# Hybrid decoder layer on one core: expert down products moved behind their own gate products, and the end of the last layer norm shared out anew

## Chip, cores and metric

One Trainium2 chip, of which the program uses one core. The metric is the time of one execution on the device in microseconds (us); lower is better. What a measurement of this kernel can tell from no change is given in the prediction.

## What is computed

The reference is one decoder layer over 512 tokens of width 1024, in float32. Attention and a spatial gating unit feed an output projection, then `x <- LN(alpha*x + mix)`. The part that this case is about comes after it: a mixture of 32 experts, of which each token uses two, and the second layer norm.

```python
def hierarchical_moe(h, ...):
    # top-1 of 4 groups, then top-2 of its 8 experts: gate (tokens, groups, experts), two entries a token
    y = jnp.zeros((B * S, D), jnp.float32)
    for g in range(N_GROUPS):
        gu = jnp.einsum('td,edf->tef', t, w_gate_up[g])
        a, b = gu[..., :EXPERT_FF], gu[..., EXPERT_FF:]
        act = jax.nn.silu(a) * b * gate[:, g, :, None]
        y = y + jnp.einsum('tef,efd->td', act, w_down[g])
    return y
...
h = layer_norm(DEEPNORM_ALPHA * h + moe, ln2_g, ln2_b)    # mean, variance, scale, shift over 1024
```

## The kernel before

**Expert pairs.** The 32 experts are worked off as 16 pairs. Each expert has 64 places for tokens, so a pair fills the 128 partitions. The weights of a pair are six tiles of 1 MB: four for the gate and up product (two halves of the depth for each of the two experts) and two for the down product. All 96 tiles come in this order over SP's queue into a ring of 20 slots (`wfill`, `slots`, L499 to L529). A slot is filled again as soon as its last product is through; up to eight transfers are under way, and SP issues the next when the eighth before it has landed.

**One turn of the loop over pairs** (L1136 to L1161) for pair p. `gate_up` (L894) multiplies gathered tokens by the gate and up weights in eight steps k; steps 0 to 3 need the first two tiles, 4 to 7 the other two. Between the steps stands other work: at k 1 the activation of pair p-1 is transposed (`act_transposed`, L1080), at k 3 `down(p - 1)` (L1089) multiplies it by the down weights, at k 4 and 5 the tokens of pair p+1 are transposed (L1071), at k 5 `fetch` picks and gathers the tokens of pair p+3. After the loop `gated` (L1074) makes silu(a)*b*gate on ScalarE and VectorE. So the down product of a pair runs in the middle of the next pair's gate products, from the down tiles that came before them. Only for the last pair, 15, `down(14)` is done before the gate products.

**Rows out and back.** ScalarE copies one half of a pair's down result out of PSUM and VectorE the other (L1101); GpSimd then writes the rows to a DRAM scratch `y_dram` by an indirect transfer (L1107): plane 0 for a token's first expert, plane 1 for its second. After the loop both planes are read back, four blocks of 128 tokens, eight transfers of 512 KB on SP (L1168); they wait for the rows of pair 14.

**The end.** Pair 15 does not go through DRAM. Its result is kept as a rounded part and a rest, `y`, and a one-hot matrix `G` spreads it over the tokens. Per block of 128 tokens and half of the width TensorE adds up in one PSUM bank: x (`fin_x`, L1197), pair 15 (`fin_y`, L1201) and the sum of the two planes (`fin_rows`, L1209). VectorE adds the planes (L1206) and takes their row sum with it. The mean of a row is put together from three sums: that of x (L1155, one block in each of pairs 11 to 14), that of pair 15 (L1238) and that of the planes (L1206, L1207). Then `ln2_scale`: ScalarE squares both halves with the mean as bias (L1214) and takes the root of the variance (L1215, L1216), VectorE subtracts the mean and multiplies by the gain (L1218). `ln2_out`: VectorE takes the reciprocal (L1222), multiplies and adds the shift (L1225), SP writes the result. Gain and shift are spread over 128 partitions by four products with 4 rows (L1175), loaded as a small tile `lnr` (L1142).

TensorE's order is written out by hand, as are those of VectorE, ScalarE, GpSimd and SP from the output projection on; waits follow from the tiles.

Of the kernel before, what the change touches and what calls it, by code (L numbers as in the profile page):

```python
# [21 lines left out]
S = 512  # L22
# [9 lines left out]
SUMMED = (NPAIR - 1,)  # L32
# [24 lines left out]
def layer(tc, I, out):  # L57
# [1031 lines left out]
    def down(p, aT, dp=None):  # L1089

        dp = dp or [ps_acc() for _ in range(2)]
        y = [wk.tile([128, D], F32R, name="y", bufs=2) for _ in range(2 if p in SUMMED else 1)]
        for n in range(2):
# [6 lines left out]
            if p not in SUMMED:  # L1100
                (dve.tensor_copy if n else act.copy)(y[0][:, ns].bitcast(F32), dp[n])  # L1101
            else:
                act.activation(y[0][:, ns], dp[n], AF.Copy, accum_out=rs[:, 2 * n:2 * n + 1])
                dve.scalar_tensor_tensor(y[1][:, ns], dp[n], 1.0, y[0][:, ns].bitcast(F32), op0=ALU.mult, op1=ALU.subtract,
                                         accum_out=rs[:, 2 * n + 1:2 * n + 2])
        if p not in SUMMED:
            pool_e.indirect_dma_start(out=y_dram[:, :], out_offset=bass.IndirectOffsetOnAxis(ap=tos[p][:, 0:1], axis=0),  # L1107
                                      in_=y[0].bitcast(F32), in_offset=None, bounds_check=2 * S - 1, oob_is_err=False)
        wfill(6 * p + 6 + NSLOT)
        return y  # L1110
# [60 lines left out]
    ln2 = slots[0]().rearrange("p (a d) -> p a d", a=2)  # L1171
    ln2_g, ln2_b = ln2[:, 0], ln2[:, 1]
    for j in range(4):
        b = ps_t().rearrange("p a b -> p (a b)")
        pe.matmul(b, ident[0:4, j:j + 1].to_broadcast([4, 128]), lnr[0:4], start=True, stop=True)  # L1175
        act.copy(ln2[:, j // 2, j % 2 * 512:j % 2 * 512 + 512], b)
    aT = act_transposed(sa)

# [7 lines left out]
    rs = mo.tile([128, 4], F32, name="rs")  # L1186
# [149 lines left out]
```

## Time and profile before

| | |
|---|---|
| three timed runs | 516.08, 517.49, 517.2 us, median 517.2 us |
| profiled execution | 520.19 us, of which 518.5 us from the first to the last instruction (the span) |
| busy share of the span | TensorE 92%, VectorE 44%, ScalarE 29%, GpSimd 23% |
| chain that ended last | TensorE 57%, transfers 31% (gate and up weights alone 20%), VectorE 7% |
| transfers | 141.18 MB, 272 GB/s over the span, 411 to 425 GB/s in slices 22 to 35 of the 40 (272 to 454 us) |

The times of the rows count from the first instruction of the profiled execution. Such an execution is longer than a timed run, so differences are worked out within it and then set against the median. PE is TensorE, PEld its weight load, DVE VectorE, ACT ScalarE, POOL GpSimd, SPq the queue of the sync engine. The granted clock is TensorE's: 1.00 is 2.4 GHz, 0.50 is 1.2 GHz. A float32 product of 128x512 shows as two records.

### The profile page before, as it was taken

What the parts mean: (1) busy time and instruction counts of PE and PEld (TensorE: products, weight loads), DVE (VectorE), ACT (ScalarE), POOL (GpSimd) and SP (SyncE); (2) the same over time, 40 slices, a digit from 0 to 9 for tenths busy, and PEclk for the clock granted to TensorE, in tenths of its full rate; (3) what the DMA queues carried; (4) which work ended last, traced back from release to release, by engine and by line L of the source; (5) the groups of instructions that cost most, each with busy time, mean ns of one, the idle gap of its engine ahead of it and who ended that gap; (6) DMA issues with size and microseconds to landing.
All of it is one profiled execution on the core that took longest, in us unless ns stands there. A gap on an engine that the chain in (4) does not pass through costs nothing.

```text
span 518.5 us, 6540 instructions
## 1 busy us (share of the span) xinstructions
PE 476.4 (92%) x2314; PEld 280.3 (54%) x2314; DVE 229.1 (44%) x588; ACT 150.4 (29%) x321; POOL 117.5 (23%) x186
## 2 busy tenths in 40 slices
PE   6999999999799999979999999999979799689971
PEld 4788887888677678769443333333313233133440
DVE  2586648624667457995532222222212322020166
ACT  4543446241668423123111111111101110012241
POOL 4024443000478511243111111111101110002000
PEclk9999999999989999998899999999979999799897
DMA  8734221930595478594589999999999999984513
GB/s 266 265 119 123 82 82 40 300 106 0 187 417 139 165 234 334 203 361 166 178 328 411 424 417 417 420 422 420 418 423 425 419 421 421 425 371 149 227 40 126
DMA packets 40748, 141.18 MB, mean 272 GB/s; under 512 B 10455, under 2 KB 14595, under 8 KB 28936
## 3 DMA queue, kind: packets, MB, share of 16 engines
q1 hardware_dynamic: 35816, 130.72, 65.8%
q0 software_dynamic: 4896, 10.00, 5.4%
q8 instruction: 20, 0.33, 0.2%
q14 instruction: 16, 0.13, 0.1%
HBM read 131.78 MB, written 16.25 MB: 286 GB/s over the span
## 4 chain that ended last, share of the span: by engine, by line
PE 57%; DMA 31%; DVE 7%; SPq 1%; issue 1%; ACT 1%; DVEq 0%; ACTq 0%
DMA wc<-in_w_gate_up 20%; PE acc L898 9%; PE acc L318 7%; PE acc L320 7%; PE acc L319 7%; PE acc L1099 5%; DMA wc<-in_w_down 4%; DMA wc19b<-in_w_down 4%; PE acc L913 3%; DMA x_sb<-in_x 2%; PE tp L613 2%; PE acc L598 1%; PE acc L573 1%; PE acc L575 1%; PE acc L574 1%
## 5 line engine op out<-in xcount | busy, mean ns | idle before, releaser
L898 PE MATMUL acc<-wc,xTm 128*64 128x512 f32 x456 | 126.6, 618 | 12.7 <-DMA wc<-in_w_gate_up 12.5
L898 PEld LDWEIGHTS acc<-wc,xTm 128*64 128x64 f32 x456 | 31.9, 139 | 68.8 <-issue 49.8
L318 PE MATMUL acc<-w_hi,xTh 128*128 128x512 f32 x160 | 64.9, 406 | 2.0 <-ACT w_hi L309 1.1
L319 PE MATMUL acc<-w_lo,xTh 128*128 128x512 f32 x160 | 62.8, 393 | 0.5 <-DVE w_lo L310 0.5
L320 PE MATMUL acc<-w_hi,xTl 128*128 128x512 f32 x160 | 62.8, 392 | 0.0
L1099 PE MATMUL acc<-wc,aT 128*64 128x512 f32 x248 | 57.7, 593 | 0.5 <-ACT aT L1086 0.5
L1101 DVE COPY y<-acc 128x512 f32<-128x512 f32 x15 | 10.4, 692 | 107.8 <-PE acc L1099 107.8
L1107 POOL DMA_INDIRECT y_dram<-y,to x15 | 15.1, 1009 | 157.3 <-DVE y L1101 157.3
L310 DVE TENSOR_TENSOR w_lo<-w_raw,w_hi 128x512 fp32r<-128x512 f32 x40 | 28.2, 706 | 35.8 <-ACT w_hi L309 35.6
L309 ACT ACTIVATE w_hi<-w_raw 128x512 fp32r<-128x512 f32 x40 | 25.3, 632 | 54.6 <-PE acc L320 47.9
L1099 PEld LDWEIGHTS acc<-wc,aT 128*64 128x64 f32 x248 | 18.1, 137 | 36.9 <-issue 36.2
L420 POOL TENSOR_TENSOR P<-P,st 128x128 f32<-128x128 f32 (+3 forms) x32 | 23.3, 748 | 52.3 <-DVE st L419 50.7
L318 PEld LDWEIGHTS acc<-w_hi,xTh 128*128 128x128 f32 x160 | 30.2, 189 | 9.1 <-ACT w_hi L309 1.8
L319 PEld LDWEIGHTS acc<-w_lo,xTh 128*128 128x128 f32 x160 | 30.1, 188 | 6.9 <-DVE w_lo L310 1.4
L320 PEld LDWEIGHTS acc<-w_hi,xTl 128*128 128x128 f32 x160 | 30.0, 188 | 6.8 <-DVE xTl L161 0.4
L1072 ACT COPY xTm<-tp 128x512 f32<-128x512 f32 x15 | 8.8, 587 | 68.1 <-PE tp L1071 68.1
L1071 PEld LDWEIGHTS tp<-ident,xg 128*128 128x128 f32 x120 | 15.5, 193 | 23.5 <-issue 13.0
L890 POOL DMA_INDIRECT xg<-h_dram,ti x15 | 15.7, 1049 | 44.7 <-issue 22.9
L866 DVE TENSOR_TENSOR sel<-iota_v,slotp 128x1024 bf16<-128x1024 f32 (+2 forms) x23 | 22.5, 990 | 0.1
L1101 ACT COPY y<-acc 128x512 f32<-128x512 f32 x15 | 8.8, 586 | 46.9 <-PE acc L1099 46.9
L1077 DVE SCALAR_TENSOR_TENSOR sa<-sa,tg,acc 128x256 f32<-128x256 f32 x16 | 7.7, 480 | 32.3 <-ACT sa L1076 28.5
L1071 PE MATMUL tp<-ident,xg 128*128 128x128 f32 x120 | 21.0, 299 | 0.0
(327 smaller groups left out, 751.5 us busy)
## 6 DMA issues: line engine op xcount, KB each, us to landing
wc<-in_w_gate_up SPq DMA_DIRECT2D x61, 1024.0 KB, 20.9
wc<-in_w_down SPq DMA_DIRECT2D x31, 1024.0 KB, 19.2
w_raw<-in_w_in SPq DMA_DIRECT2D x18, 512.0 KB, 3.9
y_dram<-zeros SPq DMA_DIRECT2D x8, 512.0 KB, 8.2
wo_raw<-in_w_out SPq DMA_DIRECT2D x16, 256.0 KB, 4.3
wc<-y_dram SPq DMA_DIRECT2D x6, 512.0 KB, 5.8
x_sb<-in_x SPq DMA_DIRECT2D x8, 256.0 KB, 5.9
h_dram<-x_sb SPq DMA_DIRECT2D x4, 512.0 KB
```

Of the source, the lines that this page charges most:

```text
L309: act.activation(wh, raw, AF.Copy)
L310: dve.tensor_tensor(wl, raw, wh.bitcast(F32), op=ALU.subtract)
L318: pe.matmul(acc[i], xh, wh, start=(k == 0), stop=False)
L319: pe.matmul(acc[i], xh, wl, start=False, stop=False)
L320: pe.matmul(acc[i], xl, wh, start=False, stop=(k == KD - 1))
L420: pool_e.tensor_tensor(P[:, 0:n], P[:, 0:n], bc(st4[:, 2:3], [128, n]), op=ALU.mult)
L866: dve.tensor_tensor(sels[p][:, 2 * a:2 * b], bc(iota_v.rearrange("p a b -> p (a b)")[:, None, :], [128, n, 128]), bc(slotp[:, p, a:b].rear ...
L890: pool_e.indirect_dma_start(out=xgs[p % 2], out_offset=None, in_=h_dram[:, :], in_offset=bass.IndirectOffsetOnAxis(ap=tis[p][:, 0:1], axis=0),
L898: pe.matmul(gp[zs], xT[k // 4][:, k % 4, zs], w[k % 4 // 2][:, k % 2 * 512:k % 2 * 512 + 512], start=(k == 0), stop=(k == KD - 1))
L1071: pe.transpose(out=tp[:, j], in_=xv[:, kk * 4 + j], identity=ident)
L1099: pe.matmul(dp[n][zs], aT[:, c, zs], w[c][:, ns], start=(c == 0), stop=(c == 1))
L1101: (dve.tensor_copy if n else act.copy)(y[0][:, ns].bitcast(F32), dp[n])
```

## The change

1. From pair 9 on (`ATONCE`) `down(p)` stands right behind `gated` of the same pair p, ahead of the gate products of pair p+1. In pair 9's turn both `down(8)`, at k 3, and `down(9)`, after the loop, are done. For pairs 1 to 8 nothing moves.
2. Rows go out without their mean: for pairs 0 to 14 ScalarE copies both halves of the down result and sums them as it goes, VectorE forms minus the mean and adds it to the 1024 columns in place, then GpSimd writes the rows. x loses its mean in the same way, one block in each of pairs 9 to 12 (three VectorE instructions in place of one). So the row mean at the end is that of pair 15 alone.
3. The planes are added by GpSimd for blocks 0 to 2 (1024 columns, no sum) and by VectorE for block 3.
4. x goes into PSUM early: `fin_x(2, ...)` ahead of pair 15's gate products, `fin_x(0, 0)` and `fin_x(1, 0)` around the transposition of pair 15's activation, `fin_x(0, 1)` and `fin_x(1, 1)` behind the first `fin_y`.
5. The small tile with gain and shift is loaded by GpSimd's queue at the start of pair 14's turn, and its four products stand in pair 14's gate products, after k 6.
6. The last layer norm is reshared: for blocks 0 and 1 ScalarE multiplies by the reciprocal and GpSimd adds the shift; for blocks 2 and 3 VectorE does both, with the value in between kept in PSUM. Block 1 is scaled before VectorE adds the planes of block 3.
7. `wfill(2 + NSLOT)` is called four gate steps earlier in pair 0. SP's own list of instructions is the same at that place.

```diff
@@ pair_out, gate_up of pair 0 @@
-        if p not in SUMMED:
+        if p < LAST:
...
         gate_up(0, xT0, k, gp)
+        if k == 3:
+            wfill(2 + NSLOT)
@@ def down(p, aT, dp=None) @@
-        y = [wk.tile([128, D], F32R, name="y", bufs=2) for _ in range(2 if p in SUMMED else 1)]
+        y = [wk.tile([128, D], F32R, name="y", bufs=2) for _ in range(2 if p == LAST else 1)]
+        y0 = y[0].bitcast(F32)
+        rs = mo.tile([128, 4], F32, name="rs", bufs=2)
...
-            if p not in SUMMED:
-                (dve.tensor_copy if n else act.copy)(y[0][:, ns].bitcast(F32), dp[n])
+            if p < LAST:
+                act.activation(y0[:, ns], dp[n], AF.Copy, accum_out=rs[:, n:n + 1])
...
-        if p not in SUMMED:
+        if p < LAST:
+            dve.tensor_scalar(rs[:, 2:3], rs[:, 0:1], rs[:, 1:2], -1.0 / D, op0=ALU.add, op1=ALU.mult)
+            dve.tensor_scalar(y0, y0, rs[:, 2:3], None, op0=ALU.add)
             pool_e.indirect_dma_start(out=y_dram[:, :], ...
@@ loop over pairs @@
-        if p == LAST:
-            down(p - 1, act_transposed(sa))
+        if p == LAST - 1:
             lnr = slots[3]().rearrange("p (a d) -> p a d", a=4)[:, 0]
             for z, n in enumerate(("ln2_g", "ln2_b")):
-                sp.dma_start(out=lnr[2 * z:2 * z + 2], in_=I[n].rearrange("o (a d) -> (o a) d", a=2))
+                pool_e.dma_start(out=lnr[2 * z:2 * z + 2], in_=I[n].rearrange("o (a d) -> (o a) d", a=2))
+        if p == LAST:
+            for n in range(2):
+                fin_x(2, n)
...
-            if k == 1 and p < LAST:
+            if k == 1 and p <= ATONCE:
                 aT = act_transposed(sa)
             if k == 3:
-                if p < LAST:
+                if p <= ATONCE:
                     down(p - 1, aT)
...
-            if k == 6 and LAST - NT <= p < LAST:
-                i = p - LAST + NT
-                dve.tensor_reduce(st2[:, i, 7:8], x_sb[:, i], axis=AX.X, op=ALU.add)
+            if k == 6 and LAST - 2 - NT <= p < LAST - 2:
+                i = p - LAST + 2 + NT
+                t = st2[:, i]
+                dve.tensor_reduce(t[:, 5:6], x_sb[:, i], axis=AX.X, op=ALU.add)
+                dve.tensor_scalar(t[:, 5:6], t[:, 5:6], -1.0 / D, None, op0=ALU.mult)
+                dve.tensor_scalar(x_sb[:, i], x_sb[:, i], t[:, 5:6], None, op0=ALU.add)
...
+            if k == 6 and p == LAST - 1:
+                for j in range(4):
+                    b = ps_s()
+                    pe.matmul(b, ident[0:4, j:j + 1].to_broadcast([4, 128]), lnr[0:4], start=True, stop=True)
+                    act.copy(ln2[:, j // 2, hs[j % 2]], b)
         wfill(6 * p + 4 + NSLOT)
         sa = gated(gp, tgs[p][:, 1:2])
+        if ATONCE <= p < LAST:
+            down(p, act_transposed(sa))
@@ the end @@
+    fin_x(0, 0)
     aT = act_transposed(sa)
+    fin_x(1, 0)
...
-        dve.scalar_tensor_tensor(rb[i][0], rb[i][0], 1.0, rb[i][1], op0=ALU.mult, op1=ALU.add, accum_out=t[:, 5:6])
-        dve.scalar_tensor_tensor(t[:, 6:7], t[:, 5:6], -1.0 / D, nx[:, i:i + 1], op0=ALU.mult, op1=ALU.add)
+        if i < NT - 1:
+            pool_e.tensor_tensor(rb[i][0], rb[i][0], rb[i][1], op=ALU.add)
         for n in range(2):
-            pe.matmul(fin[i, n], ident, rb[i][0][:, hs[n]], start=False, stop=True)
+            r = rb[i][0][:, hs[n]]
+            if i == NT - 1:
+                dve.tensor_tensor(r, r, rb[i][1][:, hs[n]], op=ALU.add)
+            pe.matmul(fin[i, n], ident, r, start=False, stop=True)
...
             o = o_sb[i][:, hs[n]]
-            dve.scalar_tensor_tensor(o, o, t[:, 4:5], ln2_b[:, hs[n]], op0=ALU.mult, op1=ALU.add)
+            if i < 2:
+                act.activation(o, o, AF.Copy, scale=t[:, 4:5])
+                pool_e.tensor_tensor(o, o, ln2_b[:, hs[n]], op=ALU.add)
+            else:
+                dve.scalar_tensor_tensor(o, fin[i, n], t[:, 4:5], ln2_b[:, hs[n]], op0=ALU.mult, op1=ALU.add)
...
     ln2_out(0)
+    ln2_scale(1)
     fin_rows(3)
-    for i in range(1, NT):
+    ln2_out(1)
+    for i in (2, 3):
```

How the instructions stand on the engines that matter, at three places. TensorE from the last gate steps of pair 15 to its first down product, before (L898 gate product, L1175 gain and shift, L1084 transposition of the activation, L1197 `fin_x`, L1099 down product):

```order
L898 MATMUL acc<-wc_3609,xTm 64x512
L1175 MATMUL tp<-wc_3785,ident 128x512 x4
L1084 MATMUL sc<-ident,sa 128x128 x2
L1197 MATMUL acc<-x_sb,ident 128x512 x2
L1197 MATMUL sc<-x_sb,ident 128x512 x2
L1197 MATMUL tp<-x_sb,ident 128x512 x2
L1099 MATMUL acc<-wc_3648,aT 64x512
```

The same place now (L900, L1088, L1151 and L1105 are the lines of the gate product, the transposition, `fin_x` and the down product):

```order
L900 MATMUL acc<-wc_3653,xTm 64x512
L1151 MATMUL acc<-x_sb,ident 128x512
L1088 MATMUL sc<-ident,sa 128x128 x2
L1151 MATMUL sc<-x_sb,ident 128x512
L1105 MATMUL acc<-wc_3694,aT 64x512
```

Ten products of 512 columns stood there beside the transposition; two are left. The others stand now further ahead or behind the down product. TensorE from pair 14's last gate steps to pair 15's first, now (L1075 transposition of pair 15's tokens, L1189 the products with gain and shift):

```order
L1075 MATMUL tp<-ident,xg_2354 128x128 x4
L900 MATMUL acc<-wc_3560,xTm 64x512
L900 MATMUL acc<-wc_3562,xTm 64x512
L1189 MATMUL sc<-wc_3782,ident 128x512 x4
L1088 MATMUL sc<-ident,sa 128x128 x2
L1105 MATMUL acc<-wc_3605,aT 64x512
L1151 MATMUL tp<-x_sb,ident 128x512 x2
L900 MATMUL acc<-wc_3636,xTm 64x512
```

Before, pair 14's gate products were followed by the transposition, `down(14)` and pair 15's gate products, and held `down(13)` in their middle. Now `down(13)` stands ahead of them, and the four products and two `fin_x` lie on the way from pair 14 to pair 15. ScalarE in the last layer norm, blocks 0 and 1, before (L1214 squares, L1215 and L1216 root of the variance):

```order
L1214 ACTIVATE wc_3845,st_2628<-acc,st_2628 128x512 x2
L1215 ACTIVATE st_2628<-st_2628,eps_3846 128x1
L1216 ACTIVATE st_2628<-st_2628 128x1
L1214 ACTIVATE wc_3845,st_2628<-sc,st_2628 128x512 x2
L1214 ACTIVATE wc_3845,st_2628<-tp,st_2628 128x512 x2
```

The same now (L1235 squares, L1236 and L1237 root, L1249 multiplication by the reciprocal):

```order
L1235 ACTIVATE wc_3908,st_2628<-acc,nx 128x512 x2
L1236 ACTIVATE st_2628<-st_2628,eps_3909 128x1
L1237 ACTIVATE st_2628<-st_2628 128x1
L1249 ACTIVATE wc_3906<-wc_3906,st_2628 128x512 x2
L1235 ACTIVATE wc_3908,st_2628<-sc,nx 128x512 x2
L1235 ACTIVATE wc_3908,st_2628<-tp,nx 128x512 x2
```

Two multiplications that wait for VectorE's reciprocal now stand between the squares of one block and those of the next, for blocks 0 and 1.

## Rows read from the trace of the kernel before

**Rows 1.** Busy time by stage: stretch, length, then PE, PEld, DVE, ACT, POOL, PEclk, DMA share, GB/s.

```profile
430.00:450.00 20.00, 15.13 (x60) 4.96 (x58) 2.99 (x4) 1.93 (x4) 1.01 (x1) 0.92 1.02 422
```

**Rows 2.** Timeline of SP's queue, weight transfers: start, length, instruction.

```profile
437.29 0.33 SPq L527 DMA_DIRECT2D wc<-in_w_down  x1
448.41 0.33 SPq L527 DMA_DIRECT2D wc<-in_w_gate_up  x1
453.32 0.33 SPq L527 DMA_DIRECT2D wc<-in_w_down  x1
```

**Rows 3.** Timeline of PE, pairs 14 and 15: start, length, instruction, records, idle time before.

```profile
448.44 3.68 PE L898 MATMUL acc<-wc,xTm 128*64 128x512 f32 x6 [1.58 <-DMA wc<-in_w_gate_up]
...
458.27 1.02 PE L898 MATMUL acc<-wc,xTm 128*64 128x512 f32 x4
...
461.51 1.94 PE L898 MATMUL acc<-wc,xTm 128*64 128x512 f32 x8
...
465.50 3.65 PE L1099 MATMUL acc<-wc,aT 128*64 128x512 f32 x16 [0.52 <-ACT aT L1086]
468.98 1.46 PE L898 MATMUL acc<-wc,xTm 128*64 128x512 f32 x6
```

**Rows 4.** Timeline of PE from pair 15's last gate product to the end.

```profile
475.95 3.77 PE L1175 MATMUL tp<-wc,ident 4*128 4x512 f32 x8
...
486.93 3.65 PE L1099 MATMUL acc<-wc,aT 128*64 128x512 f32 x16
...
496.93 1.88 PE L1209 MATMUL acc<-wc,ident 128*128 128x512 f32 x4
...
498.65 1.88 PE L1209 MATMUL sc<-wc,ident 128*128 128x512 f32 x4
```

**Rows 5.** Timeline of ACT and DVE in the last layer norm.

```profile
498.00 0.69 ACT L1214 ACTIVATE wc<-acc,st 128x512 f32<-128x512 f32 x1 [6.67 <-PE acc L1209]
...
499.44 0.19 ACT L1214 ACTIVATION_READ_ACCUMULATOR wc<-acc,st 128x1 f32 x1
...
499.67 1.41 DVE L1218 SCALAR_TENSOR_TENSOR wc<-acc,st,wc 128x512 f32<-128x512 f32 x2 [2.42 <-ACT wc L1214]
...
512.18 0.15 DVE L1222 RECIPROCAL st<-st 128x1 f32<-128x1 f32 x1
512.37 1.42 DVE L1225 SCALAR_TENSOR_TENSOR wc<-wc,st,wc 128x512 f32<-128x512 f32 x2
```

**Rows 6.** Groups by shape: busy, mean ns of one, idle before.

```profile
L309 ACT ACTIVATE w_hi<-w_raw 128x512 fp32r<-128x512 f32 x40 | 25.3, 632 | 54.6 <-PE acc L320 47.9 <-DMA w_raw<-in_w_in 4.9 <-issue 1.7
L727 ACT ACTIVATE x_sb<-x_sb,mv 128x512 f32<-128x512 f32 x5 | 3.9, 808 | 0.0
L310 DVE TENSOR_TENSOR w_lo<-w_raw,w_hi 128x512 fp32r<-128x512 f32 x40 | 28.2, 706 | 35.8 <-ACT w_hi L309 35.6
L731 POOL TENSOR_TENSOR x_sb<-x_sb,ln_b 128x512 f32<-128x512 f32 x5 | 7.0, 1400 | 0.4
```

**Rows 7.** Busy time and granted clock, columns as in rows 1.

```profile
453.00:454.00 1.00, 1.00 (x6) 0.16 (x4) 0.00 (x0) 0.21 (x1) 0.00 (x0) 0.75 0.99 418
480.00:481.00 1.00, 1.00 (x5) 0.49 (x4) 0.00 (x0) 0.98 (x3) 0.00 (x0) 0.90 0.99 389
481.00:482.00 1.00, 1.00 (x3) 0.48 (x2) 0.00 (x0) 0.92 (x1) 0.00 (x0) 0.50 1.04 373
484.00:485.00 1.00, 1.00 (x3) 0.38 (x2) 0.00 (x0) 0.00 (x0) 0.00 (x0) 0.89 1.05 430
```

**Rows 8.** Transfers issued by POOL: line, count, size, median us to landing.

```profile
lb<-in_b_expert POOLq DMA_DIRECT2D x1, 16.0 KB, 6.4
y_dram<-y,to POOLq DMA_INDIRECT x15, 8.3
```

**Rows 9.** Timeline: rows of pair 14 out, and back from DRAM.

```profile
470.64 0.98 POOL L1107 DMA_INDIRECT y_dram<-y,to  x1 [9.69 <-DVE y L1101]
474.83 3.12 SPq L1168 DMA_DIRECT2D wc<-y_dram  x6
```

More of the change, by code (lines that the diff above doesn't have):

```diff
@@ L30 @@
 NPAIR = NE // 2
-SUMMED = (NPAIR - 1,)
+LAST = NPAIR - 1
+ATONCE = 9
 FF = 256
@@ L1132, in layer, with fin_x @@
     fetch(3)
-    LAST = NPAIR - 1
     st2 = mo.tile([128, NT, 8], F32, name="st2")
+    fin = {}
+    hs = [slice(0, 512), slice(512, D)]
+    def fin_x(i, n):
+        if (i, n) not in fin:
+            fin[i, n] = (ps_acc, ps_s, ps_t, ps_acc)[i]()
+            if i == 2:
+                fin[i, n] = fin[i, n].rearrange("p a b -> p (a b)")
+        pe.matmul(fin[i, n], ident, x_sb[:, i, hs[n]], start=True, stop=False)
     for p in range(1, NPAIR):
         gp = ps_acc()
-        if p == LAST:
-            down(p - 1, act_transposed(sa))
+        if p == LAST - 1:
             lnr = slots[3]().rearrange("p (a d) -> p a d", a=4)[:, 0]
             for z, n in enumerate(("ln2_g", "ln2_b")):
-                sp.dma_start(out=lnr[2 * z:2 * z + 2], in_=I[n].rearrange("o (a d) -> (o a) d", a=2))
+                pool_e.dma_start(out=lnr[2 * z:2 * z + 2], in_=I[n].rearrange("o (a d) -> (o a) d", a=2))
+            ln2 = slots[0]().rearrange("p (a d) -> p a d", a=2)
+            ln2_g, ln2_b = ln2[:, 0], ln2[:, 1]
+        if p == LAST:
+            for n in range(2):
+                fin_x(2, n)
         for k in range(KD):
@@ L1170, in layer @@
     G = one_hot(LAST)
[L1171 to L1176, printed above, removed]
+    dp = [ps_acc() for _ in range(2)]
+    fin_x(0, 0)
     aT = act_transposed(sa)
+    fin_x(1, 0)
     o2 = [slots[z]().rearrange("p (a d) -> p a d", a=2) for z in (1, 2)]
@@ L1185, in layer @@
     act.preload_act_table(AF.Sqrt)
-    rs = mo.tile([128, 4], F32, name="rs")
     nx = mo.tile([128, NT], F32, name="nx")
-    dp = [ps_acc() for _ in range(2)]
-    fin = {}
-    hs = [slice(0, 512), slice(512, D)]
-    def fin_x(i, n):
-        if (i, n) not in fin:
-            fin[i, n] = (ps_acc, ps_s, ps_t, ps_acc)[i]()
-            if i == 2:
-                fin[i, n] = fin[i, n].rearrange("p a b -> p (a b)")
-        pe.matmul(fin[i, n], ident, x_sb[:, i, hs[n]], start=True, stop=False)
     def fin_y(i, n):
@@ L1203, in fin_rows @@
     def fin_rows(i):
[L1205 to L1207 removed]
+        if i < NT - 1:
+            pool_e.tensor_tensor(rb[i][0], rb[i][0], rb[i][1], op=ALU.add)
         for n in range(2):
[L1209 removed]
+            r = rb[i][0][:, hs[n]]
+            if i == NT - 1:
+                dve.tensor_tensor(r, r, rb[i][1][:, hs[n]], op=ALU.add)
+            pe.matmul(fin[i, n], ident, r, start=False, stop=True)
     def ln2_scale(i):
         t = st2[:, i]
+        m = nx[:, i:i + 1]
         for n in range(2):
[L1214 removed]
+            act.activation(sq[:, 2 * (i % 2) + n], fin[i, n], AF.Square, bias=m, accum_out=t[:, n:n + 1])
         act.activation(t[:, 2:3], t[:, 0:1], AF.Identity, bias=eps2, scale=1.0 / D)
@@ L1224, in ln2_out @@
             o = o_sb[i][:, hs[n]]
-            dve.scalar_tensor_tensor(o, o, t[:, 4:5], ln2_b[:, hs[n]], op0=ALU.mult, op1=ALU.add)
+            if i < 2:
[3 more added lines that the diff above has]
+                dve.scalar_tensor_tensor(o, fin[i, n], t[:, 4:5], ln2_b[:, hs[n]], op0=ALU.mult, op1=ALU.add)
             sp.dma_start(out=out_d[:, i, hs[n]], in_=o)
-    for i in range(NT - 1):
-        for n in range(2):
-            fin_x(i, n)
-    y = down(LAST, aT, dp)
+    y, rs = down(LAST, aT, dp)
     for i in range(NT - 1):
         fin_y(i, 0)
+    fin_x(0, 1)
+    fin_x(1, 1)
     fin_x(NT - 1, 0)
```

12 lines of the change are left out of this document (5 added, 7 removed).

## The prediction

> **What bounds the kernel now.** I read the page first (engine shares and the 40 slices), then the busy times by stage, the chain of waits, the timelines of TensorE and of SP's queue from 430 us on, and last the timelines of ScalarE and VectorE in the final layer norm.
>
> The stages differ. From about 360 us to pair 14 the weights decide: in 20 us there TensorE is busy for 15.1, while the transfers are busy throughout [rows 1]. SP issues a weight transfer when the eighth before it has landed, so the issues date the landings: 437.3 is the landing of pair 13's last gate tile, 448.4 of pair 14's second, 453.3 of its last [rows 2]. TensorE's gate products start at 448.44, with the second tile there [rows 3]. Behind pair 14 TensorE decides: gate products of pair 15 until 475.95, 11.0 us until its down product, 10.0 us from there to the first sum with the planes [rows 4]. Then ScalarE and VectorE decide: squares from 498.00, results until 513.79 [rows 5], and 4.7 us for the last transfer and the closing.
>
> So an edit in pairs 9 to 13 is worth little by itself. What is moved on the path from the landing at 453.3 to the end is worth its full length.
>
> **Step 1, pair 14 to the end of pair 15's gate products.** Down(13) now stands ahead of pair 14's gate products. Pair 13's gate products can end 5.2 us after 437.3 (the second half of a pair's gate products takes 5.2 us with the transpositions in it, from 458.27 to 463.45). With 2.05 us from the last gate product to the down product (463.45 to 465.50) and 3.5 for it (465.50 to 468.98) [rows 3] down(13) ends at 448.0, ahead of the landing at 448.4: it costs nothing. From 453.3 the path is 5.2 (second half) + 3.7 (four products with gain and shift, from 3.77 us for eight records [rows 4]) + 2.05 + 3.5 (down(14)) + 1.7 (two `fin_x`, as long as the pair at 496.93, which is followed at 498.65 [rows 4]) + 7.0 (pair 15's gate products, 468.98 to 475.95 [rows 3, 4]). That is 23.1 us, so 476.4 against 475.95: **+0.45**. What is late next if the weights come later is the same landing.
>
> **Step 2, to the down product of pair 15.** 11.0 us before. Now 2.4: the wait of 2.05, with one `fin_x` under it, and what the second one, behind the transposition, sticks out (0.35). **−8.6**.
>
> **Step 3, to the first sum with the planes.** 10.0 us before; two `fin_x` are moved behind the first `fin_y`: **+1.7**. GpSimd's additions are taken at nothing: two times 1.40 us for 1024 columns [rows 6], 2.8 a block. Pair 14's rows leave when they did (470.6), the reads back begin at 474.8 and issue in 3.1 us [rows 9]; blocks then land about every 2.4 us (1 MB at 422 GB/s, rows 1), the first at about 482, and GpSimd ends block 0 near 485 and block 2 near 490.4, while the first sum, which needs block 0 alone, is due at 476.4 + 2.4 + 11.7 = 490.5. If that cover goes, the rows from DRAM are late next, and each us is a us.
>
> **Step 4, the last layer norm.** From the first sum to VectorE's last result 16.9 us before (496.93 to 513.79, rows 4 and 5). Now ScalarE has more to do. I count from the first sum's start: squares and sums of block 0 end at 2.7 (499.44 + 0.19 less 496.93), scaled by 4.15 (1.41 for two), reciprocal 4.3 (0.15); two multiplications on ScalarE at 0.63 each [rows 6], the nearest shape of 512 columns without a per-column operand, to 5.6; squares of block 1 to 7.25, scaled by 8.7; VectorE's two additions for block 3 at 0.71 [rows 6] to 10.1; reciprocal and two multiplications to 11.55; squares of block 2 to 13.2; then VectorE alone, two blocks of 1.41 + 0.15 + 1.42 [rows 5], to 19.2. **+2.3**. By 0.81 us for each multiplication (L727's form, rows 6) it would be 0.7 more, and with slower additions 3.3 in all; with values read from PSUM as quickly as now not under 2.2.
>
> **Step 5, the clock.** TensorE's granted clock fell to 0.50 behind the four 4-row products: 0.90 in the microsecond from 480, 0.50 in the next, and it was back in that from 484, with the engine listed as busy throughout [rows 7]. It had also been low at 453 (0.75 there), after the stall ahead of 448.44. These products now stand on the path, ahead of down(14). Some 3.4 us at half clock cost 1.7 of work; in the kernel before they fell on `fin_x`, which was on the path too, inside the 11.0 us that step 2 takes as removed. So they come back in another place: **+1.7**, between 0 (no fall) and 3.4 (a spell of twice the length, as the one that ended at 453).
>
> The Trainium skill ("TensorE: Matmul & The Clock Gate", Part 1) ties the clock to how busy the engine has been. By it, products that run without a gap would cost nothing and the sum would be 1.7 us lower; the fall at 481 behind gapless products is against that reading here.
>
> **Step 6, gain and shift.** Their two small loads stand on GpSimd's queue behind pair 13's rows, which now leave after down(13): 448.0, + 0.8 and about 1.6 (ScalarE's last copy with its sum, and VectorE's addition in place; from the 512-column forms of rows 6), and about 1 for the issue [rows 9], so 451.5. A small load of GpSimd's took 6.4 us to land, rows 8.3 [rows 8]: there at 458 to 460. TensorE wants them behind step 6 of pair 14, at 457.7 or a little later. I take **+0.5**, nearest to the 6.4 us row, which is of the same kind; bounds 0 and 3.
>
> **At nothing.** The mean of pairs 0 to 14 (VectorE twice 512 columns in place, ScalarE the second copy too): VectorE is busy 3.0 and ScalarE 1.9 of 20 us [rows 1], and nobody on the path waits for these rows but those of 13 and 14, counted above. If cover went, it would be 0.7 to 1.4 us a pair. x without its mean: three instructions on the same idle VectorE. The 2-us wait ahead of each down product of pairs 9 to 13 lies in TensorE's 4.9 us idle out of 20. The rows of pair 13 leave earlier, half a megabyte, 1.2 us of transfers at most, in the range. `wfill` moved: SP's list is the same.
>
> **Sum.** 0.45 − 8.6 + 1.7 + 2.3 + 1.7 + 0.5 = −1.95, so −2.0 us within the profiled execution (520.19 us, span 518.5), which is 3.0 us longer than the median of the three runs, 517.2. Set against the median: **515.2 us**.
>
> **The rivals.**
>
> - *The clock holds and the loads are in time.* Steps 5 and 6 fall away: −4.15, 513.0 us. For it: TensorE has fewer gaps behind 453.3 than it had. Against it: the fall at 481 [rows 7]. 0.15.
> - *The small loads arrive late, and the clock falls for long.* One mechanism at one place, in front of the four products: TensorE stands still there for up to 3 us, ahead of products that already cost it the clock, and pair 14's activation and down product and all of pair 15 wait behind it in order. Price: 2.5 more than step 6 and 1.7 more than step 5, so +2.2: 519.4 us. It decides from a landing later than about 459.5, which is 8 us after issue, less than the 8.3 us of the rows ahead in that queue [rows 8]. For it: that order of the queue. Against: 16 KB landed in 6.4. 0.22.
> - *The path is shortened but given back.* TensorE's 8.6 us return elsewhere: the rows of the planes, or the ScalarE turns in the layer norm at their upper price (+1.0), and the small loads 1 us later than step 6 has them: −2.0 + 1.0 + 1.0 = 0, 517.2 us. For it: no row shows ScalarE's multiplication by a per-row operand in this place, and GpSimd's 2.8 us a block are longer than the 2.4 between blocks. Against: the rows nearest to both are the ones that the sum uses. 0.23.
>
> A rule that speaks against the moved sums is in the Trainium skill ("SBUF — State Buffer", the "DVE blocks DMA" trap): while VectorE uses the port it shares with GpSimd, GpSimd cannot write its transfers' descriptors. By it the additions in place would delay the gathers of the next pairs by their own 0.7 to 1.4 us; no row of this case shows such a delay.
>
> **How the numbers follow.** The forecast has 0.40: between 1 and 3 us less. A measurement of this kernel can tell about 0.3%, 1.55 us, from no change. Of the forecast about 0.27 lies beyond that and 0.13 within; the first rival is faster by more (0.15); the second is slower (0.20 of 0.22 beyond the bound); the third is within, with 0.03 on the faster and 0.02 on the slower side. That gives 0.45 faster, 0.33 the same, 0.22 slower. The range of 8 in 10 goes from 512.6, the first rival with its lower bounds, to 519.0, just short of the second's centre. The likeliest case's own range is 514.2 to 516.2.
>
> **What would show it.** Step 1: the last gate product of pair 15 ends near 476.4 plus what steps 5 and 6 cost, up to 479. Step 2: its down product begins 2.4 us later. Step 3: the first sum with the planes starts 11.7 us after that, and no wait for GpSimd stands before it. Step 4: VectorE's last result 19 us after the first sum. Step 5: a granted clock of 0.50 soon after the 4-row products. Step 6: the wait ahead of these products, 0 to 3 us, put down to the two small loads. Pairs 10 to 13: waits of the gate products for transfers, as before. I would be wrong if the weights themselves came later (another rate, or SP held up), if the clock fell over a longer stretch in pairs 9 to 13, where the waits now fall between gate and down products, or if rows of pair 14 came back so late that the first sum waits.

## The result, and the profile after

| | before | changed |
|---|---|---|
| median of the timed runs | 517.2 us (515.47 to 517.49, five runs) | 522.02 us (520.48 to 522.69, five runs) |
| ratio | | 1.010, 95% interval 1.0074 to 1.0125: slower by 1% |
| profiled execution | 520.19 us, span 518.5 | 522.02 us, span 520.2 |
| busy: TensorE, VectorE, ScalarE, GpSimd | 92, 44, 29, 23% | 92, 44, 32, 25% |
| pair 15's last gate product ends | 475.95 [rows 4] | 483.96 |
| its down product begins | 486.93 [rows 4] | 486.32 |
| first sum with the planes | 496.93 [rows 4] | 498.05 |
| VectorE's last result | 513.79 [rows 5] | 516.16 |

The time was lost ahead of pair 15's last gate product. Timeline of TensorE in the changed kernel (start, length, instruction, records, idle time before), to be held against [rows 3, 4]:

```profile
452.20 1.07 PE L900 MATMUL acc<-wc,xTm 128*64 128x512 f32 x2 [0.83 <-DMA wc<-in_w_gate_up]
...
455.49 1.08 PE L900 MATMUL acc<-wc,xTm 128*64 128x512 f32 x4
458.99 6.69 PE L1189 MATMUL sc<-wc,ident 4*128 4x512 f32 x8 [2.42 <-DMA wc<-in_ln_b]
465.61 1.98 PE L900 MATMUL acc<-wc,xTm 128*64 128x512 f32 x4
...
469.83 5.27 PE L1105 MATMUL acc<-wc,aT 128*64 128x512 f32 x16 [0.52 <-ACT aT L1090]
...
476.94 7.09 PE L900 MATMUL acc<-wc,xTm 128*64 128x512 f32 x32
483.96 1.12 PE L1151 MATMUL acc<-x_sb,ident 128*128 128x512 f32 x2
...
486.32 3.65 PE L1105 MATMUL acc<-wc,aT 128*64 128x512 f32 x16
...
498.05 1.88 PE L1229 MATMUL acc<-wc,ident 128*128 128x512 f32 x4
```

TensorE stands still for 2.42 us behind the gate product of 455.49, for the shift. The four products then take 6.69 us, where the same eight records took 3.77 before [rows 4]; the last gate step takes 1.98 in place of 1.08, and down(14) 5.27 in place of 3.65. Busy time by stage of the same kernel (columns as in rows 1) shows the clock:

```profile
452.00:456.50 4.50, 4.30 (x18) 1.62 (x18) 0.69 (x1) 0.59 (x1) 0.00 (x0) 1.00 1.02 428
456.50:459.00 2.50, 0.08 (x3) 0.05 (x1) 0.00 (x0) 0.00 (x0) 0.00 (x0) 1.00 1.02 421
459.00:465.60 6.60, 6.60 (x8) 2.20 (x8) 0.00 (x0) 1.76 (x3) 0.00 (x0) 0.54 0.76 321
465.60:469.70 4.10, 2.68 (x7) 0.61 (x6) 0.48 (x1) 1.27 (x3) 0.00 (x0) 0.50 0.20 84
469.70:473.00 3.30, 3.17 (x8) 1.01 (x10) 0.00 (x0) 0.07 (x1) 0.00 (x0) 0.50 0.07 27
473.00:475.00 2.00, 2.00 (x10) 0.42 (x6) 0.00 (x0) 0.69 (x2) 0.00 (x0) 0.97 0.00 0
```

The granted clock is 1.00 up to the products, 0.50 from within them until about 473, some 13.6 us. GpSimd's timeline shows when the loads were issued:

```profile
449.63 0.99 POOL L1115 DMA_INDIRECT y_dram<-y,to  x1 [15.97 <-DMA wc<-in_w_down]
...
451.20 0.56 POOL L1159 DMA_DIRECT2D wc<-in_ln_b  x1
```

The shift was issued at 451.20, behind pair 13's rows, and landed 7.65 us later by the chain of waits, 458.85. TensorE wanted it at 456.57.

### The profile page after: what moved, and what is told of

It is laid out like the page before. It is cut to its first block, busy times and chain, and to the rows that moved or that the text cites. A ratio compares the mean times of both kernels' runs of the same rounds, so it can differ in the third digit from the quotient of the medians.

```text
span 520.2 us, 6621 instructions
## 1 busy us (share of the span) xinstructions
PE 477.1 (92%) x2314; PEld 280.8 (54%) x2314; DVE 229.0 (44%) x596; ACT 164.5 (32%) x370; POOL 131.2 (25%) x195
## 4 chain that ended last, share of the span: by engine, by line
PE 55%; DMA 32%; DVE 7%; ACT 2%; issue 1%; SPq 1%; POOL 1%; POOLq 0%; ACTq 0%; DVEq 0%
DMA wc<-in_w_gate_up 20%; PE acc L900 7%; PE acc L320 7%; PE acc L321 7%; PE acc L322 7%; PE acc L1105 4%; DMA wc<-in_w_down 4%; DMA wc19b<-in_w_gate_up 4%; PE acc L915 3%; DMA x_sb<-in_x 2%; DMA wc<-in_ln_b 1%; PE acc L600 1%; PE tp L615 1%; PE acc L575 1%; PE sc L1189 1%
## 5 line engine op out<-in xcount | busy, mean ns | idle before, releaser
L900 PE MATMUL acc<-wc,xTm 128*64 128x512 f32 x456 | 120.3, 606 | 3.3 <-DMA wc<-in_w_gate_up 3.0
L1105 PE MATMUL acc<-wc,aT 128*64 128x512 f32 x248 | 63.0, 632 | 3.1 <-ACT aT L1090 3.1
L900 PEld LDWEIGHTS acc<-wc,xTm 128*64 128x64 f32 x456 | 32.5, 137 | 58.2 <-issue 45.9
L1113 DVE TENSOR_SCALAR rs<-rs 128x1 f32<-128x1 f32 x15 | 3.2, 214 | 94.5 <-ACT y L1107 94.5
L1105 PEld LDWEIGHTS acc<-wc,aT 128*64 128x64 f32 x248 | 18.9, 145 | 41.6 <-issue 36.4
L1107 ACT ACTIVATE y<-acc 128x512 f32<-128x512 f32 x30 | 17.9, 597 | 61.3 <-PE acc L1105 61.3
L1075 PEld LDWEIGHTS tp<-ident,xg 128*128 128x128 f32 x120 | 15.5, 194 | 23.5 <-issue 16.2
L892 POOL DMA_INDIRECT xg<-h_dram,ti x15 | 15.7, 1047 | 44.5 <-issue 22.6
L1075 PE MATMUL tp<-ident,xg 128*128 128x128 f32 x120 | 21.0, 299 | 0.0
```

The costliest lines, as they stand in the source:

```text
L900: pe.matmul(gp[zs], xT[k // 4][:, k % 4, zs], w[k % 4 // 2][:, k % 2 * 512:k % 2 * 512 + 512], start=(k == 0), stop=(k == KD - 1))
L1075: pe.transpose(out=tp[:, j], in_=xv[:, kk * 4 + j], identity=ident)
L1105: pe.matmul(dp[n][zs], aT[:, c, zs], w[c][:, ns], start=(c == 0), stop=(c == 1))
L1107: act.activation(y0[:, ns], dp[n], AF.Copy, accum_out=rs[:, n:n + 1])
```

## The experiments

The numbers that are compared: the time, and in the profile the **path**, from the first product of pair 14's second half (it starts with the landing of its last gate tile) to the end of pair 15's last gate product, which is the start of the `fin_x` behind it. In the changed kernel it is 483.96 − 452.20 = 31.8 us. Each path is that of one profiled execution. Medians of different runs are set against the kernel before on the same chip (518.0 to 518.2 us there, 517.2 for the changed kernel itself), as ratios with 95% intervals.

### The kernel before once more

No edit.

> The kernel before once more, with a profile of its own. The three timed runs (median 517.2 us) were 3.0 us shorter than the profiled execution (520.19). Theory: the profiled execution had two spells of half clock from 440 us on (446.7 to 453.5 and 480.8 to 484.2), and others lack one: then this profile has a span of 515 to 516.5 us and fewer or shorter spells from 440 us on, with the same pieces between them (11.0 us from pair 15's last gate product to its down product less 1.7 where the spell is missing). Rival: every profiled execution of this kernel is about 3 us longer than a timed one, then the span is 518 to 519 again with the same spells.

Measured: 518.07 against 518.01 us, ratio 1.001 (0.998 to 1.004); profiled execution 518.06, span 516.4. TensorE's timeline, and the clock by stage:

```profile
472.24 4.64 PE L1175 MATMUL tp<-wc,ident 4*128 4x512 f32 x8
...
484.81 3.65 PE L1099 MATMUL acc<-wc,aT 128*64 128x512 f32 x16
```

```profile
472.00:476.80 4.80, 4.80 (x10) 1.36 (x8) 0.48 (x1) 2.14 (x4) 0.00 (x0) 0.81 0.61 211
476.80:481.80 5.00, 5.00 (x9) 2.41 (x9) 0.00 (x0) 2.24 (x3) 0.00 (x0) 0.50 0.96 368
```

The span came as the theory had it (516.4 in 515 to 516.5), but not for its reason: it looked for the missing spell in the wrong place. Behind the 4-row products there is one here too, and a longer one (0.50 from about 475.0 to 481.8, and 12.6 us between gate and down product in place of 11.0). The rival falls: this profiled execution lies on the median of its runs. The spells that are missing stand much earlier. Busy time by stage of the first profile of before, and of this one:

```profile
130.00:155.00 25.00, 22.00 (x123) 17.17 (x122) 16.07 (x61) 16.65 (x49) 15.45 (x19) 0.93 0.79 305
222.00:255.00 33.00, 29.61 (x162) 24.50 (x162) 23.56 (x77) 8.71 (x14) 11.72 (x10) 0.84 0.65 227
```

```profile
130.00:155.00 25.00, 21.68 (x134) 17.01 (x133) 17.29 (x67) 17.53 (x53) 15.47 (x20) 1.00 0.80 308
222.00:255.00 33.00, 29.61 (x164) 23.47 (x163) 23.40 (x75) 7.17 (x11) 11.52 (x10) 0.90 0.64 226
```

A mean clock of 0.93 against 1.00 in 25 us, 0.84 against 0.90 in 33: each missing hundredth costs its hundredth of the stretch, so up to 1.75 and 2.0 us. The same steps of TensorE lie 0.3 us apart in the two executions at 150 us, 1.5 at 153, 2.05 at 255, and still 2.0 at the landing of pair 14's last gate tile, by the last weight issue (451.3 here against 453.3 [rows 2]). So 2.0 us of the two spells' loss reach the landing. Over 25 runs the kernel before took 514.95 to 521.49 us; the first profile lies in the upper part of that.

### Load early or late, 4 rows or 128

Four kernels that differ in two things alone: the changed kernel; one with the load a pair earlier; one with that and full products; one with the late load and full products. The edit for the early load:

```diff
-        if p == LAST - 1:
-            lnr = slots[3]().rearrange("p (a d) -> p a d", a=4)[:, 0]
+        if p == LAST - 2:
+            lnr = slots[16]().rearrange("p (a d) -> p a d", a=4)[:, 0]
...
+        if p == LAST - 1:
```

and for the full products:

```diff
+            dve.memset(lnr, 0.0)
...
-                    pe.matmul(b, ident[0:4, j:j + 1].to_broadcast([4, 128]), lnr[0:4], start=True, stop=True)
+                    pe.matmul(b, ident[:, j:j + 1].to_broadcast([128, 128]), lnr, start=True, stop=True)
```

> The changed kernel, with gain and shift loaded one pair earlier by the same queue; the four 4-row products stay where they are. In the changed kernel TensorE waited 2.42 us for these loads and was then at half clock from 459.5 to 473.1; pair 15's last gate product ended at 484.03, where the path without wait and without half clock comes to about 475.5. Theory (the 4-row products bring the clock down and hold it down): no wait, but a granted clock of 0.50 a few us after the first of these products, for 3.4 us or more; gate products of pair 15 end at 477 to 480, 516 to 518 us. Rival (the wait alone brought the clock down): no 0.50 between 452 and 476, end of gate products at 475 to 476, 513.5 to 514.5 us. Second rival (the wait was hidden and the loss lies elsewhere): 521 to 522.

> As the run with the early load, with the four products on 128 rows (the rows beyond the fourth are zero) in place of 4: same columns, same place. Theory (4 rows are what counts): 1.00 all through from 452 to 476, end of pair 15's gate products at 475 to 476, 513.5 to 514.5 us. Rival (the wait alone): the same 513.5 to 514.5, but then the early load with 4 rows shows it too. Second rival (the clock falls there whatever the products are): as the early load with 4 rows, with a spell of 0.50 behind the products, 516 to 518.

> The changed kernel with its late small loads, so that TensorE waits (about 2.4 us, and some 0.5 for the zeros that are written first), and with the four products on 128 rows. Theory (4 rows hold the clock down; the wait can bring it down, and full rows bring it back): one spell of 0.50 of about 3.4 us behind the wait, or none; the four products in 3.8 to 6 us; pair 15's last gate product 2.4 to 5 us behind the path without wait; 516 to 518.5 us. Rival (the wait alone brings the long spell): half clock from the wait on for over 10 us, as in the changed kernel, 521 to 523.

Timelines of TensorE, and the clock by stage. Early load, 4 rows:

```profile
450.50 1.07 PE L900 MATMUL acc<-wc,xTm 128*64 128x512 f32 x2 [0.87 <-DMA wc<-in_w_gate_up]
...
454.80 3.77 PE L1190 MATMUL sc<-wc,ident 4*128 4x512 f32 x8
...
461.82 6.00 PE L1105 MATMUL acc<-wc,aT 128*64 128x512 f32 x16 [0.52 <-ACT aT L1090]
...
476.69 1.12 PE L1151 MATMUL acc<-x_sb,ident 128*128 128x512 f32 x2
```

```profile
458.50:461.80 3.30, 1.78 (x7) 0.51 (x6) 0.48 (x1) 1.34 (x3) 0.00 (x0) 0.69 0.82 348
461.80:467.70 5.90, 5.88 (x16) 1.62 (x16) 0.00 (x0) 0.69 (x2) 0.00 (x0) 0.59 0.37 156
```

Early load, 128 rows (the clock is 1.00 from 452.0 to 475.6):

```profile
451.97 1.07 PE L900 MATMUL acc<-wc,xTm 128*64 128x512 f32 x2 [0.88 <-DMA wc<-in_w_gate_up]
...
456.27 3.78 PE L1191 MATMUL sc<-wc,ident 128*128 128x512 f32 x8
...
463.11 3.65 PE L1105 MATMUL acc<-wc,aT 128*64 128x512 f32 x16 [0.52 <-ACT aT L1090]
...
475.62 1.12 PE L1151 MATMUL acc<-x_sb,ident 128*128 128x512 f32 x2
```

Late load, 128 rows:

```profile
453.41 1.07 PE L900 MATMUL acc<-wc,xTm 128*64 128x512 f32 x2 [0.84 <-DMA wc<-in_w_gate_up]
...
460.26 5.42 PE L1190 MATMUL sc<-wc,ident 128*128 128x512 f32 x8 [2.47 <-DMA wc<-in_ln_b]
...
468.74 3.65 PE L1105 MATMUL acc<-wc,aT 128*64 128x512 f32 x16 [0.52 <-ACT aT L1090]
...
481.25 1.13 PE L1151 MATMUL acc<-x_sb,ident 128*128 128x512 f32 x2
```

```profile
460.20:465.60 5.40, 5.34 (x8) 1.92 (x8) 0.00 (x0) 1.75 (x3) 0.00 (x0) 0.68 0.82 346
465.60:468.70 3.10, 1.60 (x7) 0.51 (x6) 0.48 (x1) 1.34 (x3) 0.00 (x0) 1.00 0.39 164
```

| | load late | load early |
|---|---|---|
| 4 rows | path 31.8; 522.02 us, 1.010 (1.0074 to 1.0125) | path 26.2; 516.71, 0.997 (0.994 to 1.000) |
| 128 rows | path 27.8; 516.98, 0.998 (0.996 to 1.000) | path 23.65; 513.37, 0.990 (0.987 to 0.994) |

Both causes exist. Without either the path is 23.65 us at full clock. The 4 rows alone cost 2.5: the products themselves run at full speed (3.77), and the clock falls behind them, to 0.50 from about 459.8 to 466.6, so that down(14) takes 6.00. The wait alone costs its 2.47 and 1.7 of clock: 0.50 from about 460.4 to 463.8, within the products, which take 5.42; it is back before they end, and down(14) takes 3.65. Each of the two is clear of noise in the time as well (0.997 and 0.998 against 0.990). Together they cost 8.1: 2.42 of wait and 5.7 of clock.

That is 1.4 us more than 2.5 and 4.2. Whether the two feed each other is not shown by it: each path is one execution, and in the kernel before the 4 rows cost 1.9 us in one execution and 3.5 in the other (11.0 and 12.6 us to the down product, where full rows take 9.1, as a later run shows). In the ratios the excess is 0.005, no more than the four intervals leave open.

The theories that were written first in the three expectations held: 516.7 for 516 to 518, 513.4 for 513.5 to 514.5 (0.1 below it), 517.0 for 516 to 518.5. The rivals that blamed the wait alone fall, as the early load with 4 rows has a spell of 0.50 and no wait, and the late load with full rows has a short one only.

### No products at all

```diff
+            for z, n in enumerate(("ln2_g", "ln2_b")):
+                sp.dma_start(out=ln2[:, z], in_=I[n].to_broadcast([128, D]))
...
-                for j in range(4):
-                    b = ps_s()
-                    pe.matmul(b, ident[0:4, j:j + 1].to_broadcast([4, 128]), lnr[0:4], start=True, stop=True)
-                    act.copy(ln2[:, j // 2, hs[j % 2]], b)
```

The two transfers stand at the start of pair 15's turn, where SP has issued all weights; the small loads go.

> The changed kernel without the four products and the small loads: gain and shift are spread over the partitions by two transfers of 512 KB on SP's queue behind the last weights. Theory: wait (2.4), products (6.7 at half clock) and the half clock behind them (some 3) all go: pair 15's gate products end at 471.5 to 473, if its weights are there, and the end moves with it: 510 to 512 us. Rival (the 12 us are given back: pair 15's last weights or pair 14's rows from DRAM are late next): TensorE waits for them, 514 to 517 us.

Measured: 510.13 us, ratio 0.986 (0.979 to 0.992), from four runs between 506.14 and 512.06. TensorE's timeline:

```profile
448.60 1.07 PE L900 MATMUL acc<-wc,xTm 128*64 128x512 f32 x2 [0.81 <-DMA wc<-in_w_gate_up]
...
468.40 1.12 PE L1151 MATMUL acc<-x_sb,ident 128*128 128x512 f32 x2
```

The path is 19.8 us, that of the full early products less 3.85, their own length. Nothing waits for the weights or the rows of pair 14 in exchange, as the theory said.

The landing itself lay between 448.6 us (here) and 453.4 (late load with full rows), in programs that are the same up to pair 13. That is the scatter between executions that the second profile of the kernel before shows, so paths are compared here, and not instants.

### The kernel before, with full products, and without any

The same two edits in the kernel before (`dve.memset` and 128 rows; or the two spreading transfers on SP and no products), at the places where it has them.

> The kernel before with its four products on 128 rows in place of 4 (the others zero), in the place where they stood. Theory (also there the 4 rows bring the clock down): no 0.50 between the last gate product of pair 15 and its down product; 9 to 9.5 us between them in place of 11.0 and 12.5; 515 to 516.5 us. Rival (the clock falls there for another reason): a spell of 0.50 again, 518.

> The kernel before, without its four 4-row products: gain and shift are spread by two transfers of 512 KB on SP's queue behind the last weights, as in the changed kernel without products (510.1 us against 518.0 before). Theory (the products and their half clock cost the kernel before some 5 us, and the rest of the change is worth some 3): from pair 15's last gate product to its down product some 7 us in place of 11.0 and 12.5, no granted clock of 0.50 there, 512 to 514 us. Rival (the rest of the change brings nothing, all of the gain over before is the products): 510 to 511 us. Second rival (in the kernel before the products are hidden): 517 to 518.

Measured: full products 516.93 us, ratio 0.996 (0.993 to 0.998); none 514.09, ratio 0.992 (0.989 to 0.994). TensorE's timeline and the clock with full products:

```profile
474.70 3.78 PE L1176 MATMUL tp<-wc,ident 128*128 128x512 f32 x8
...
483.79 3.65 PE L1099 MATMUL acc<-wc,aT 128*64 128x512 f32 x16
```

```profile
474.70:478.40 3.70, 3.70 (x11) 1.54 (x10) 0.48 (x1) 2.14 (x4) 0.00 (x0) 1.00 0.92 345
```

Where the clock was 0.81 and 0.50 with 4 rows it is 1.00, and the way to the down product takes 9.1 us in place of 11.0 and 12.6. So the half clock there came with the 4 rows, in a stretch without a wait. Without products it is 6.6 us. The kernel before lost 4 us to them. The rest of the change was worth 4.0 by the medians (514.09 to 510.13), whose intervals overlap, and 2.4 by the profiles: from the landing of pair 14's last gate tile to VectorE's last result it is 54.4 us in the kernel before without products (453.4 to 507.8) and 52.0 in the changed one (448.6 to 500.6).

### What the down products' place is worth

The changed kernel without products, with `ATONCE = 14`: the down products of pairs 9 to 13 stand in the next pair's gate products again.

> The changed kernel without products, with the down products of pairs 9 to 13 back in the middle of the next pair's gate products; only down(14) follows its own pair. Theory (the move takes down(13) out of pair 14's turn, where it would stand between the landing of pair 14's second tile and its last gate products): pair 14's second half of gate products starts 2 to 3.5 us after the landing of its last gate tile, and the time is 2 to 3.5 us above that of the kernel without products (510.1). Rival (transfers cover it either way): within 1 us of it.

Measured: 513.39 us, ratio 0.991 (0.989 to 0.993), against 0.986 with the move. SP's queue and TensorE:

```profile
447.57 2.76 SPq L529 DMA_DIRECT2D wc<-in_w_down  x2
```

```profile
454.85 1.02 PE L900 MATMUL acc<-wc,xTm 128*64 128x512 f32 x4
```

The second of the two weight transfers ends its issue at 450.3, so pair 14's last gate tile had landed at about 450.0; the second half starts at 454.85, behind down(13). That is 4.85 us lost at this place in this execution, more than the 2 to 3.5 expected. In the time it is 3.3 by the medians, whose intervals overlap, so the profile carries the reading.

About half of the 4.85 is clock. The granted clock was 0.50 from 443.2 to 450.0 here, in and behind the stalls ahead of pair 14's first gate products (2.96 and 1.91 us); TensorE worked 4.9 us of that, which is an estimate of 2.4 us lost. All five profiles with down(13) inside pair 14's gate products (the three of the kernel before with products, the one without, and this one) have such a spell there, of 3.4 or 6.8 us, and the loss behind the landing is 3.2 us with the short one and 4.85 to 5.2 with the long one. In the eight profiles with down(13) moved ahead, the clock is 1.00 from 430 to the landing. So the move fills a stall, and with it goes this spell.

### The last layer norm

On the kernel without products: the sharing of before (VectorE for all four blocks, with the order of the calls of before and the value in between in SBUF throughout); or the sum of block 3's planes earlier; or both. The main lines of the two edits:

```diff
-            if i < 2:
-                act.activation(o, o, AF.Copy, scale=t[:, 4:5])
-                pool_e.tensor_tensor(o, o, ln2_b[:, hs[n]], op=ALU.add)
-            else:
-                dve.scalar_tensor_tensor(o, fin[i, n], t[:, 4:5], ln2_b[:, hs[n]], op0=ALU.mult, op1=ALU.add)
+            dve.scalar_tensor_tensor(o, o, t[:, 4:5], ln2_b[:, hs[n]], op0=ALU.mult, op1=ALU.add)
```

```diff
-    ln2_scale(0)
     fin_rows(2)
+    fin_rows(3)
+    ln2_scale(0)
     ln2_out(0)
-    fin_rows(3)
```

> The changed kernel without products, and with the last layer norm shared out as before: VectorE multiplies and adds for all four blocks, ScalarE's multiplications and GpSimd's additions of blocks 0 and 1 are gone, block 3's planes are added where they were before. Theory (the resharing costs: from the first sum with the planes to VectorE's last result it took 18.1 us in the changed kernel and 16.9 before): 15.5 to 17 us for that stretch in place of 18.1, and the time 1 to 2.5 us below that of the kernel without products (510.1). Rival (the resharing pays, as VectorE has 4 products of 512 columns more here): 19 us or more, 511 to 513 us.

> The changed kernel without products, with the sum of block 3's planes on VectorE ahead of the first block's scaling, where VectorE waits for some 4 us; its two products with it. Theory (this sum, 1.28 us between block 1's scaling and its reciprocal, holds up ScalarE's multiplication and with it the squares of blocks 2 and 3): 1.3 us less from the first sum to VectorE's last result (18.1), about 508.8 us. Rival (ScalarE or the rows from DRAM hold the chain): within 0.4 us of the kernel without products, or later by the wait for block 3's rows.

> The two edits that paid, together: the changed kernel without products, the last layer norm shared out as before (506.25 us), and the sum of block 3's planes ahead of the first block's scaling. Theory (VectorE holds the chain there without a gap from the first scaling on, so that the 1.28 us of the sum leave it, less what the wait for block 3's rows pushes back): 1.0 to 1.3 us less, 505 us, and the fastest of all runs. Rival (the squares on ScalarE, two blocks ahead, hold it then): within 0.4 us of 506.25.

| on the kernel without products | first sum to VectorE's last result | time | ratio to before |
|---|---|---|---|
| as changed | 18.1 us | 510.13 us | 0.986 (0.979 to 0.992) |
| sum of block 3 early | 16.9 | 507.27 | 0.979 (0.975 to 0.984) |
| sharing of before | 15.4 | 506.25 | 0.977 (0.975 to 0.980) |
| both | 14.2 | 504.37 | 0.973 (0.970 to 0.975) |

ScalarE and VectorE of the changed kernel hand the work back and forth:

```profile
502.10 0.15 DVE L1245 RECIPROCAL st<-st 128x1 f32<-128x1 f32 x1
502.29 1.33 ACT L1249 ACTIVATE wc<-wc,st 128x512 f32<-128x512 f32 x2 [1.04 <-DVE st L1245]
...
506.31 1.28 DVE L1228 TENSOR_TENSOR wc19g<-wc19g,wc19b 128x512 f32<-128x512 f32 x2
...
507.70 1.33 ACT L1249 ACTIVATE wc<-wc,st 128x512 f32<-128x512 f32 x2 [2.23 <-DVE st L1245]
...
514.75 1.41 DVE L1252 SCALAR_TENSOR_TENSOR wc<-acc,st,wc 128x512 f32<-128x512 f32 x2
```

ScalarE waits 2.23 us for the reciprocal of block 1, which stands behind the sum of 506.31, and the squares of block 2 wait behind ScalarE. With both edits VectorE works without a stop from 487.12 on:

```profile
485.08 1.30 DVE L1221 TENSOR_TENSOR wc19g<-wc19g,wc19b 128x512 f32<-128x512 f32 x2 [2.57 <-DMA wc19b<-y_dram]
487.12 1.41 DVE L1233 SCALAR_TENSOR_TENSOR wc<-acc,nx,wc 128x512 f32<-128x512 f32 x2 [0.74 <-ACT wc L1228]
...
497.15 1.42 DVE L1241 SCALAR_TENSOR_TENSOR wc<-wc,st,wc 128x512 f32<-128x512 f32 x2
```

The resharing cost 2.7 us by its own stretch; the sum of block 3 cost 1.2 in either sharing. From the landing to the first sum all four take 33.9 us, so nothing was pushed out of the stretch. The theories of all three expectations held in the main, each by its stretch (15.5 to 17 us were expected for the old sharing, 15.4 measured; 1.3 and 1.0 to 1.3 for the sum, 1.2 measured). The times fell by more, 3.9, 2.9 and 5.8 us against 510.13; that median rests on four scattered runs, and only the version with both edits has an interval clear of its, so the stretches carry the reading for each edit alone. The version with both edits is the fastest of all runs and beats both kernels: 504.37 us, 2.7% less than before.

## Why the prediction was wrong

Forecast: 515.2 us in 512.6 to 519.0. Measured: 522.02. By its steps, within the two profiled executions:

| term | forecast | measured |
|---|---|---|
| landing of pair 14's last gate tile | 0 | −1.1 (453.3 to 452.2) |
| path to pair 15's last gate product, full clock, no wait | +0.45 (23.1 for 22.6) | +1.0 (23.65, early load with full rows) |
| step 6, wait for the small loads | +0.5, up to 3 | +2.42 |
| step 5, half clock | +1.7, up to 3.4 | +5.7 |
| step 2, to the down product | −8.6 (2.4 left) | −8.6 (2.36) |
| step 3, to the first sum | +1.7 | +1.7 (11.73) |
| step 4, last layer norm | +2.3 | +1.25 (18.1) |
| last transfer and closing | 0 | −0.7 |
| sum | −2.0 | +1.7 |

Of the 6.8 us between forecast and measurement some 3.7 lie in these terms, and 3.0 in the base.

**The step that failed is step 5**, with step 6 at its side. The mechanism was right and stood as the second rival, at a chance of 0.22 and 519.4 us: TensorE stands still ahead of the four products, and they cost it the clock. The size was wrong: 1.7 us was taken, 3.4 at most, and 5.7 measured. The bound came from the longest spell of half clock in the profile of before, 6.8 us, where the spell was now 13.6. The two-by-two table shows what was left out: the sum had a price for the 4 rows alone, which cost 2.5 us of clock here, but the wait costs clock by itself, 1.7 us with full rows. That makes 4.2 of the 5.7. The other 1.5 us stay open: at half clock the four products last 6.69 us in place of 3.77, which may have held the clock low for longer, but one program scatters as much. Without wait and with full rows the same program takes 513.4 us, where the first rival had 513.0 for that case.

Step 6 had the issue (451.5, measured 451.20) and the landing (458 to 460, measured 458.85) about right. The wait was 2.42 in place of 0.5 because the shift was wanted at 456.57, 1.1 us before the 457.7 that I had worked out, since the weights came that much earlier, and because it took 7.65 us where the sum went by 6.4, a load of 16 KB. The profile of before has a load of 4 KB on that queue, the size of these, which would have been the nearer row:

```profile
bsp<-in_b_spatial POOLq DMA_DIRECT2D x1, 4.0 KB, 7.7
```

**The second failure is the base.** Of the measured 4.8 us, 1.8 stand between the two profiled executions (520.19 and 522.02); the other 3.0 are the distance of the first profile from its own runs' median, which I noted and then subtracted the sum from the median all the same. The second profile of before lies on its median. The first profile held more half clock early on, worth 2.0 us at pair 14's last landing, in code that the change does not touch; what is worked out from one execution on a chain that begins there has to carry such a scatter in its range.

What was right: step 2 to 0.05 us, step 3 to 0.05, and the order of events in step 4, whose stages came 0 to 1.1 us earlier than the rows added up. GpSimd's additions held nothing up, as predicted: 2.36 us a block, no idle time ahead of the first sum at 498.05. The mean taken out of the rows cost 0.75 us of VectorE per pair, beside transfers. That the resharing of the layer norm loses time was right in sign: 1.25 us against the stretch before, and 2.7 against the old sharing with the new additions. The delay of the gathers that the prediction weighed stays open: from issue to landing they took 8.6 to 8.8 us by the median in the four profiles of the kernel before and its variants, 8.7 to 9.6 in the nine of the changed one. The chain that ended last in the changed kernel holds no wait for them from pair 0 on, so it cost nothing there, and no run takes the additions away alone.

Step 5 weighed a rule of the Trainium skill ("TensorE: Matmul & The Clock Gate", Part 1), by which the clock follows how busy TensorE has been recently. The fall behind the wait agrees with it, 1.7 us of clock with full rows. The fall behind 4-row products without a gap in the kernel before, gone with 128 rows, does not, if the rows of the profile are taken for busy; there the measurement decides.

## What to carry to other kernels

Four products with 4 rows kept TensorE listed as busy here and still cost it the clock, and so did a wait of 2.5 us: before such products are moved onto the path, take constants that are spread over partitions from a transfer in a gap of the queue, or use all rows. When two causes of one cost can meet at one place, price them together, and do not take the largest value seen so far for a bound. Before work is shared over more engines at the end of a program, look which engine then waits for whose turn: one engine without gaps was faster here than three that hand over.

## What the runs showed of the hardware

A VectorE instruction of 0.17 us can last as long as GpSimd's current one. In the kernel without products, GpSimd and VectorE:

```profile
478.00 2.37 POOL L1217 TENSOR_TENSOR wc<-wc 128x1024 f32<-128x1024 f32 x1 [0.21 <-DMA wc<-y_dram]
479.61 0.78 DVE L1259 TENSOR_SCALAR nx<-nx 128x4 f32<-128x4 f32 x1
```

It ends at 480.39, GpSimd's at 480.37; in four other kernels the two ends lie as close together (0.02 or 0.03 us apart, the VectorE instruction between 0.75 and 1.68 us long), and in the changed kernel, where GpSimd is idle, it takes 0.17. The Trainium skill ("SBUF — State Buffer", "SBUF: two separate sides") says that a GpSimd instruction and a VectorE instruction of a mode with two ports exclude each other on a shared pair of ports: the one that starts first has it for its whole length, and the other waits. These rows agree, if the VectorE instruction is of such a mode, which the profile does not say. Here it cost nothing, as ScalarE needs the value 3 us later.

The length of a half-clock spell is no property of its trigger: with the same four products it was 3.4 us in one execution of the kernel before and 6.8 in the other, 6.8 in the changed kernel with the early load, and 13.6 in the changed kernel, where a wait stood ahead of them. What sets the length is not shown.
